# Layer 0's MLP in the one-operand form of layer 1, and two drains moved up in priority

## The chip, the cores and the metric

One core of one Trainium2 chip runs the whole program. The metric is the time of one execution in microseconds (us), the median of the runs shown. The engines are PE (TensorE matmul; its weight loads are PEld), DVE (VectorE), ACT (ScalarE), POOL (GpSimd) and SP (SyncE, which here only issues DMAs). Each engine takes its instructions in the order in which the program was built.

## The reference, cut to what matters

Two layers over 256 tokens of width 2048. The change touches the second half of layer 0:

```python
h = rmsnorm(x, norm_mlp_w[layer]) * (1.0 + sc_m) + sh_m
x = x + g_m * (jnp.square(jax.nn.relu(h @ w_ff1[layer])) @ w_ff2[layer])
```

with `w_ff1` 2048 x 8192 and `w_ff2` 8192 x 2048. The modulation vectors (`sh_m`, `sc_m`, `g_m` and their three partners of the mixer) come from `mod = silu(c) @ ada_w[layer] + ada_b[layer]`, with `ada_w` 2048 x 12288 per layer.

## The kernel before

**Precision.** A float32 product is made of three products of rounded parts: each operand is split into a high part (rounded to fp32r) and a low part (the rest), and high x low, low x high and high x high are added up. Activations are kept transposed (features on partitions, 256 tokens along the free axis), so a weight block of 128 x 128 is the stationary operand.

**Two forms of the same sum.** `mm_b` (L278 to L280) runs three matmuls of 256 columns for a block: weight high on activation low, weight low on activation high, weight high on activation high, all into one sum of 256 columns. `mm_w` (L260, L262) keeps the high and the low part of the activation side by side as one operand of 512 columns: one matmul of 512 columns with the high weights, one of 256 columns with the low weights. Its result stands as two half sums in PSUM, which whoever reads it must add. Both stream 768 columns for a block. Layer 1's MLP uses `mm_w` (`wide=True`), layer 0's uses `mm_b`.

**Weights.** They arrive in chunks of 512 KB (8 blocks, tile `raw`, 6 buffers; DMA issued on SP). ACT rounds a chunk to its high part (`wh`, L222, 3 buffers), then DVE or POOL subtracts to get the low part (`wl`, L228, 3 buffers). In layer 0 `pool_ff1` and `pool_ff` give POOL 70 to 80% of these subtractions; in the last step of FF2 and in layer 1 DVE does all.

**Modulation beside it.** `ada_w` is multiplied on DVE: each 512 KB tile `ada` (4 buffers) takes one scalar_tensor_tensor with the conditioning vector, which stands in PSUM (L309). Where its DMA stands among the weights' DMAs, and where the product stands in DVE's row, was settled when the program was scheduled. 100 of the 192 `ada` pairs are planned into layer 0's MLP.

**The MLP stage.** FF1 and FF2 are interleaved in 8 steps: step s makes 1024 hidden features (two blocks of 512), and FF2 adds the 1024 features of step s-1 to the residual `X`. In layer 0 the first 6 FF1 blocks run in two passes over 8 of the 16 contraction tiles each, so that PE can start on the first half of the normalised activations `h` (L557, L566) before the rest is made. Even before that a "lead" block (L514 to L516) runs on activations without the norm's factor, while the norm's sum is finished. The last step of FF2 is followed by the lead of layer 1, whose operands `u` are made by `lead_u` (L473, L474, L478) from `X`, and by the sum of squares `ss` (L406, L407).

**PSUM.** Results use pool `pj`, two tiles of 1024 columns, taken in turn. A tile is free for PE again when all its readers are done. With `mm_b` a tile holds 512 output features, in FF2 the sum of 32 blocks; with `mm_w` it holds 256 features, in FF2 16 blocks. FF2's readers are residual updates (scalar_tensor_tensor of 256 columns, L862 or L1124); FF1's are ACT copies or DVE adds.

**Order.** The program is written with a tile scheduler that places instructions on each engine by priority and its own estimate of when they are ready. `high_priority(offset=URGENT)` moves a piece of code ahead; it is used for the norm chains, the lead's operands and its output.

Of the kernel before, what the change touches and what calls it, by code (L numbers as in the profile page):

```python
# [12 lines left out]
ALU = mybir.AluOpType  # L13
# [6 lines left out]
KT = 16  # L20
# [24 lines left out]

CFG = [dict(wide=False, gap=1, win=[2, 2, 2, 4, 6], late=2, lead_win=False, ada_win=[4, 4, 8, 12, 14], ada_late=4, ada_out=19,
            ff1=[8, 8], ff1_blocks=6, early_ff1=[[0, 1]], stat_ff1=(0, 1), ada_ff1=[16, 16], ada_ff=68,
# [8 lines left out]
URGENT = 400  # L56
# [7 lines left out]
class Trunk:  # L64
# [840 lines left out]
    def layer(self, l):  # L905
# [6 lines left out]
        for g, kts in enumerate(G):  # L912
# [10 lines left out]
            last = kts[-1] == KT - 1  # L923
# [55 lines left out]
        nb = cfg["ff1_blocks"]  # L979
        acc = {}  # L980
        for g, kts in enumerate(G):
# [7 lines left out]
            if led:  # L989
                acc[0] = self.slot()  # L990
                if cfg["wide"]:
                    self.lead_out(ps, acc[0])
                    acc[0] = self.square_wide(acc[0])
                elif kts[-1] == KT - 1:
                    self.lead_out(ps, acc[0], AF.Relu)
                    acc[0] = self.square(acc[0])
                else:
                    self.lead_out(ps, acc[0])
# [74 lines left out]
    def ff1_wide(self, l, b, kts, acc=None):  # L1073
# [4 lines left out]
        for h in range(2):  # L1078
# [7 lines left out]
            p0, p1 = self.sums(ps)  # L1086
            if fresh:
                nc.scalar.copy(d, p1)
            else:
                nc.vector.tensor_tensor(d, p1, d, ALU.add)  # L1090
            nc.vector.tensor_tensor(d, p0, d, ALU.add)
        return self.square_wide(t) if done else t
# [13 lines left out]
    def ff2_wide(self, l, s, hid, last):  # L1106
        V = self.nc.vector
        if last:
            self.stat_begin()
            self.per = 0.0  # L1110
        tail = last and l == DEPTH - 1
        for nb in range(6 if tail else 8):
            ps = self.pair()
            for c in range(2):
# [4 lines left out]
            for n in range(2):  # L1119
                k = 2 * nb + n  # L1120
                g = self.mod[l][:, 5 * KT + k:5 * KT + k + 1]
                with self.tc.high_priority(offset=URGENT * last):
                    for c in range(n * 512, n * 512 + 512, T):
                        V.scalar_tensor_tensor(self.X(k), ps[:, c:c + T], g, self.X(k), ALU.mult, ALU.add)  # L1124
            if last and nb % 2 == 1:
                self.stat_piece(nb // 2)
            if tail:
                for n in range(2):
                    self.final_scale(2 * nb + n)
# [154 lines left out]
```

## Time and profile before

| what | value |
|---|---|
| median of 3 runs | 2505.57 us (2504.9 to 2508.94) |
| the profiled execution's own time | 2509.01 us |
| its span, first to last instruction | 2506.9 us |
| mean granted PE clock | 0.984 |
| PE / DVE / ACT / POOL busy share | 97% / 65% / 47% / 33% |
| layer 0's MLP weights issued | 504.6 to 1257.8 us |
| layer 1's MLP weights issued | from 1737.7 us to the end |

Busy shares are of the whole span. PE's matmuls overlap in the pipeline, so a busy PE is not yet PE at its full rate: its rate is read from the starts of its matmuls. In a page's row the idle time of an engine is put down to what ended it.

### The profile page before, as it was taken

What the parts mean: (1) busy time and instruction counts of PE and PEld (TensorE: products, weight loads), DVE (VectorE), ACT (ScalarE), POOL (GpSimd) and SP (SyncE); (2) the same over time, 40 slices, a digit from 0 to 9 for tenths busy, and PEclk for the clock granted to TensorE, in tenths of its full rate; (3) what the DMA queues carried; (4) which work ended last, traced back from release to release, by engine and by line L of the source; (5) the groups of instructions that cost most, each with busy time, mean ns of one, the idle gap of its engine ahead of it and who ended that gap; (6) DMA issues with size and microseconds to landing.
All of it is one profiled execution on the core that took longest, in us unless ns stands there. A gap on an engine that the chain in (4) does not pass through costs nothing.

```text
span 2506.9 us, 42898 instructions
## 1 busy us (share of the span) xinstructions
PE 2422.3 (97%) x17064; PEld 2267.9 (90%) x17064; DVE 1634.7 (65%) x2568; ACT 1178.9 (47%) x1469; POOL 822.5 (33%) x360
## 2 busy tenths in 40 slices
PE   7999999989999999999989999999999999999997
PEld 6999888989999999999989899799888888888886
DVE  5767768696655544544488777556766766676675
ACT  4444565344634444444455466454644444344443
POOL 7887665445666666676400000000000000000000
PEclk8999999989999999999999999999999999999998
DMA  9999767889999988888667777455566666666662
GB/s 347 354 331 331 274 229 272 300 319 342 323 332 339 335 295 300 300 306 302 203 237 266 264 252 268 135 177 183 170 186 187 192 186 190 188 187 189 188 192 85
DMA packets 177233, 630.22 MB, mean 251 GB/s; under 512 B 19588, under 2 KB 24326, under 8 KB 177032
## 3 DMA queue, kind: packets, MB, share of 16 engines
q1 hardware_dynamic: 176312, 626.95, 73.2%
q8 instruction: 134, 2.20, 0.4%
q10 hardware_dynamic: 720, 0.53, 0.1%
q14 instruction: 67, 0.55, 0.1%
HBM read 625.30 MB, written 2.10 MB: 250 GB/s over the span
## 4 chain that ended last, share of the span: by engine, by line
PE 72%; DVE 5%; DMA 3%; issue 1%; ACT 0%; SPq 0%; DVEq 0%; ACTq 0%
PE pj L260 18%; PE pj L279 12%; PE pj L278 12%; PE pj L280 12%; PE pj L262 9%; DMA ada<-ada_w 2%; DVE wl L228 2%; PE pj L290 1%; PE pj L289 1%; PE pj L291 1%; DVE ada L309 1%; PE mx L686 0%; DVE blk L478 0%; PE mx L515 0%; DVE h L566 0%
## 5 line engine op out<-in xcount | busy, mean ns | idle before, releaser
L222 ACT CAST wh<-raw 128x1024 fp32r<-128x1024 f32 x804 | 840.7, 1048 | 1117.0 <-PE pj L280 522.0
L228 POOL TENSOR_TENSOR wl<-raw,wh 128x1024 fp32r<-128x1024 f32 (+1 forms) x326 | 798.2, 2453 | 396.7 <-ACT wh L222 385.6
L228 DVE TENSOR_TENSOR wl<-raw,wh 128x1024 fp32r<-128x1024 f32 x478 | 587.3, 1230 | 387.7 <-ACT wh L222 386.7
L309 DVE SCALAR_TENSOR_TENSOR ada<-ada,cond 128x1024 f32<-128x1024 f32 x380 | 455.5, 1214 | 190.4 <-DMA ada<-ada_w 188.8
L279 PE MATMUL pj<-h,wl 128*128 128x256 f32 x1952 | 559.0, 287 | 7.5 <-DVE wl L228 4.2
L278 PE MATMUL pj<-h,wh 128*128 128x256 f32 x1952 | 557.5, 286 | 7.8 <-DVE h L566 6.9
L280 PE MATMUL pj<-h,wh 128*128 128x256 f32 x1952 | 555.7, 285 | 0.0
L279 PE MATMUL pj<-blk,wl 128*128 128x256 f32 x1536 | 435.5, 284 | 5.0 <-DVE wl L228 3.0
L278 PE MATMUL pj<-blk,wh 128*128 128x256 f32 x1536 | 434.8, 283 | 2.9 <-ACT blk L604 1.5
L280 PE MATMUL pj<-blk,wh 128*128 128x256 f32 x1536 | 433.9, 283 | 0.0
L1179 POOL TENSOR_TENSOR blk<-blk,R 128x1024 f32<-128x1024 f32 x1 | 2.4, 2351 | 1267.5 <-ACT R L445 1267.5
L279 PEld LDWEIGHTS pj<-h,wl 128*128 128x128 f32 x1952 | 376.9, 193 | 10.4 <-DVE wl L228 5.5
L278 PEld LDWEIGHTS pj<-h,wh 128*128 128x128 f32 x1952 | 376.2, 193 | 8.7 <-DVE h L566 7.1
L280 PEld LDWEIGHTS pj<-h,wh 128*128 128x128 f32 x1952 | 376.7, 193 | 0.2
L260 PE MATMUL pj<-blk,wh 128*128 128x512 f32 x992 | 347.4, 394 | 0.0
L260 PE MATMUL pj<-h,wh 128*128 128x512 f32 x960 | 336.7, 395 | 3.1 <-DVE h L566 3.0
L279 PEld LDWEIGHTS pj<-blk,wl 128*128 128x128 f32 x1536 | 292.5, 190 | 5.9 <-DVE wl L228 3.6
L278 PEld LDWEIGHTS pj<-blk,wh 128*128 128x128 f32 x1536 | 292.8, 191 | 3.7 <-ACT blk L604 1.7
L280 PEld LDWEIGHTS pj<-blk,wh 128*128 128x128 f32 x1536 | 292.6, 191 | 0.0
L262 PE MATMUL pj<-blk,wl 128*128 128x256 f32 x992 | 278.4, 281 | 0.0
L262 PE MATMUL pj<-h,wl 128*128 128x256 f32 x960 | 268.9, 280 | 0.0
L260 PEld LDWEIGHTS pj<-blk,wh 128*128 128x128 f32 x992 | 186.2, 188 | 43.2
(248 smaller groups left out, 2941.0 us busy)
## 6 DMA issues: line engine op xcount, KB each, us to landing
raw<-w_ff SPq DMA_DIRECT2D x508, 512.0 KB, 4.4
ada<-ada_w SPq DMA_DIRECT2D x380, 512.0 KB, 6.6
raw<-w_in SPq DMA_DIRECT2D x224, 512.0 KB, 5.3
raw<-w_out SPq DMA_DIRECT2D x64, 512.0 KB, 4.4
X<-x SPq DMA_DIRECT2D x4, 512.0 KB, 6.7
raw<-ada_w SPq DMA_DIRECT2D x4, 512.0 KB, 9.3
raw<-w_ff SPq DMA_DIRECT2D x8, 256.0 KB, 3.4
out<-blk SPq DMA_DIRECT2D x4, 512.0 KB, 2.8
```

The costliest lines, as they stand in the source:

```text
L222: nc.scalar.copy(hi, raw)
L228: eng.tensor_tensor(lo, raw, hi.bitcast(F32), ALU.subtract)
L260: nc.tensor.matmul(o.rearrange("p (a b) -> p a b", b=T), lhsT=wh[:, s], rhs=act, start=first, stop=False, skip_group_check=True)
L262: nc.tensor.matmul(o[:, :T], lhsT=wl[:, s], rhs=act[:, 0, :], start=False, stop=last, skip_group_check=True)
L278: nc.tensor.matmul(o, lhsT=wh[:, s], rhs=al, start=st, stop=False, skip_group_check=True)
L279: nc.tensor.matmul(o, lhsT=wl[:, s], rhs=ah, start=False, stop=False, skip_group_check=True)
L280: nc.tensor.matmul(o, lhsT=wh[:, s], rhs=ah, start=False, stop=last, skip_group_check=True)
L289: nc.tensor.matmul(o, lhsT=al[:, s], rhs=wh, start=first, stop=False)
L290: nc.tensor.matmul(o, lhsT=ah[:, s], rhs=wl, start=False, stop=False)
L291: nc.tensor.matmul(o, lhsT=ah[:, s], rhs=wh, start=False, stop=last)
L309: nc.vector.scalar_tensor_tensor(raw, raw, 1.0, self.cond, ALU.mult, ALU.mult, accum_out=self.part[l][:, i, h:h + 1])
L1179: nc.gpsimd.tensor_tensor(o, o, self.R[:, None, :].to_broadcast((P, 4, T)), ALU.mult)
```

## The change

`CFG[0]["wide"]` becomes true: layer 0's MLP goes through `ff1_wide`, `ff2_wide` and `lead_w2`, and its weights are laid out in chunks of 4 contraction tiles x 256 columns (the host's layout follows the flag). Bytes, chunks, the split into high and low parts and the share of POOL stay. The lead's block is no longer squared when only half of its contraction is there, POOL's share falls to 0 in FF2's last step as it did in `ff2`, and the calls of `early` that `ff2` had are put into `ff2_wide`. Besides, residual updates of every step, and FF1's half sums, are put under `high_priority` in both layers.

```diff
-CFG = [dict(wide=False, gap=1, win=[2, 2, 2, 4, 6], late=2, lead_win=False, ada_win=[4, 4, 8, 12, 14], ada_late=4, ada_out=19,
+CFG = [dict(wide=True, gap=1, win=[2, 2, 2, 4, 6], late=2, lead_win=False, ada_win=[4, 4, 8, 12, 14], ada_late=4, ada_out=19,
...
                     self.lead_out(ps, acc[0])
-                    acc[0] = self.square_wide(acc[0])
+                    if kts[-1] == KT - 1:
+                        acc[0] = self.square_wide(acc[0])
...
             p0, p1 = self.sums(ps)
-            if fresh:
-                nc.scalar.copy(d, p1)
-            else:
-                nc.vector.tensor_tensor(d, p1, d, ALU.add)
-            nc.vector.tensor_tensor(d, p0, d, ALU.add)
+            with self.tc.high_priority(offset=URGENT):
+                if fresh:
+                    nc.scalar.copy(d, p1)
+                else:
+                    nc.vector.tensor_tensor(d, p1, d, ALU.add)
+                nc.vector.tensor_tensor(d, p0, d, ALU.add)
...
         if last:
             self.stat_begin()
+            self.pool_share = 0.0
             self.per = 0.0
...
+            if last and nb >= 6:
+                self.early(CFG[l + 1]["early_win"], nb - 6, l + 1, 0, 1)
...
-                with self.tc.high_priority(offset=URGENT * last):
+                with self.tc.high_priority(offset=URGENT):
...
                 self.stat_piece(nb // 2)
+                if nb == 7:
+                    self.early(CFG[l + 1]["early_win"], 2, l + 1, 0, 1)
```

What the engines' rows look like at three places. `pj_` and a number is one PSUM tile, `ada_` one modulation tile, `wh_`/`wl_` the parts of one weight chunk, `X_91` to `X_94` the four quarters of the residual; line numbers after the change are 2 to 5 higher from L990 on.

PE in FF1, two blocks of 128 x 128 with `mm_b` before:

```order
L278 MATMUL pj_5673<-h,wh_5682 128x256
L279 MATMUL pj_5673<-h,wl_5683 128x256
L280 MATMUL pj_5673<-h,wh_5682 128x256
L278 MATMUL pj_5673<-h,wh_5682 128x256
L279 MATMUL pj_5673<-h,wl_5683 128x256
L280 MATMUL pj_5673<-h,wh_5682 128x256
```

and three blocks with `mm_w` now, so that a block takes two weight loads and not three:

```order
L260 MATMUL pj_5850<-h,wh_5881 128x512
L262 MATMUL pj_5850<-h,wl_5882 128x256
L260 MATMUL pj_5850<-h,wh_5881 128x512
L262 MATMUL pj_5850<-h,wl_5882 128x256
L260 MATMUL pj_5850<-h,wh_5881 128x512
L262 MATMUL pj_5850<-h,wl_5882 128x256
```

DVE in FF1's first pass, up to the subtraction for the twelfth weight chunk of the MLP, before:

```order
L566 TENSOR_TENSOR h<-ht_6404,h 128x2x256
L566 TENSOR_TENSOR h<-ht_6410,h 128x2x256
L557 TENSOR_TENSOR ht_6416<-X_94,R 128x512
L309 SCALAR_TENSOR_TENSOR ada_6318,part_123<-ada_6318,cond 128x1024
L557 TENSOR_TENSOR ht_6422<-X_94,R 128x512
L228 TENSOR_TENSOR wl_5890<-raw_5887,wh_5889 128x1024
```

and the same place now (L1093 is the add of a half sum, the reader of a `pj` tile):

```order
L557 TENSOR_TENSOR ht_6276<-X_94,R 128x512
L1093 TENSOR_TENSOR blk_5673<-pj_5674,blk_5673 128x512
L557 TENSOR_TENSOR ht_6282<-X_94,R 128x512
L1093 TENSOR_TENSOR blk_5673<-pj_5727,blk_5673 128x512
L309 SCALAR_TENSOR_TENSOR ada_6169,part_123<-ada_6169,cond 128x1024
L309 SCALAR_TENSOR_TENSOR ada_6172,part_123<-ada_6172,cond 128x1024
L566 TENSOR_TENSOR h<-ht_6276,h 128x2x256
L566 TENSOR_TENSOR h<-ht_6282,h 128x2x256
L309 SCALAR_TENSOR_TENSOR ada_6197,part_123<-ada_6197,cond 128x1024
L228 TENSOR_TENSOR wl_5882<-raw_5879,wh_5881 128x1024
```

Counted from the start of the norm's chain to this subtraction, DVE's row holds 14 products of `ada` and not 12, 8 of L566 and not 6, and two adds of half sums that it did not hold at all.

DVE near the end of FF2's last step, before; `pj_13922` is the last tile but one, and its four updates are one row:

```order
L309 SCALAR_TENSOR_TENSOR ada_14679,part_124<-ada_14679,cond 128x1024
L309 SCALAR_TENSOR_TENSOR ada_14682,part_124<-ada_14682,cond 128x1024
L228 TENSOR_TENSOR wl_14103<-raw_14100,wh_14102 128x1024
L862 SCALAR_TENSOR_TENSOR X_93<-pj_13922,mod_125,X_93 128x256 x4
L228 TENSOR_TENSOR wl_14157<-raw_14154,wh_14156 128x1024
L309 SCALAR_TENSOR_TENSOR ada_14685,part_124<-ada_14685,cond 128x1024
```

and now; of the last four tiles `pj_12230` is the first and `pj_12279` the second, L1129 is the residual update:

```order
L1129 SCALAR_TENSOR_TENSOR X_93<-pj_12230,mod_125,X_93 128x256
L228 TENSOR_TENSOR wl_12378<-raw_12375,wh_12377 128x1024
L407 TENSOR_TENSOR ss<-ss,blk_12226 128x512
L309 SCALAR_TENSOR_TENSOR ada_12933,part_124<-ada_12933,cond 128x1024
L309 SCALAR_TENSOR_TENSOR ada_12936,part_124<-ada_12936,cond 128x1024
L1129 SCALAR_TENSOR_TENSOR X_93<-pj_12230,mod_125,X_93 128x256 x2
L228 TENSOR_TENSOR wl_12400<-raw_12397,wh_12399 128x1024
L1129 SCALAR_TENSOR_TENSOR X_93<-pj_12279,mod_125,X_93 128x256
L228 TENSOR_TENSOR wl_12427<-raw_12424,wh_12426 128x1024
L309 SCALAR_TENSOR_TENSOR ada_12939,part_124<-ada_12939,cond 128x1024
L1129 SCALAR_TENSOR_TENSOR X_93<-pj_12230,mod_125,X_93 128x256
L309 SCALAR_TENSOR_TENSOR ada_12942,part_124<-ada_12942,cond 128x1024
```

The four updates of `pj_12230` are spread over the row, the fourth behind three subtractions and three products. The tile after next on PE, `pj_12374`, takes over the place of `pj_12230` in PSUM.

## Rows read from the trace of the kernel before

**Rows 1.** The page's first part: busy us (share of the span) xinstructions.

```profile
PE 2422.3 (97%) x17064; PEld 2267.9 (90%) x17064; DVE 1634.7 (65%) x2568; ACT 1178.9 (47%) x1469; POOL 822.5 (33%) x360
```

**Rows 2.** Stretches of the span: busy us and instructions of each engine, clock, DMA.

```profile
505.00:600.00 95.00, 82.56 (x632) 80.79 (x631) 86.68 (x136) 48.00 (x72) 47.17 (x19) 0.93 0.89 322
600.00:1240.00 640.00, 640.00 (x5373) 640.00 (x5372) 322.15 (x487) 282.00 (x276) 431.90 (x176) 1.00 0.88 308
1240.00:1320.00 80.00, 72.68 (x575) 72.06 (x574) 65.12 (x124) 42.19 (x65) 0.00 (x0) 0.93 0.66 225
1740.00:2450.00 710.00, 706.34 (x4145) 621.80 (x4144) 480.65 (x623) 317.85 (x362) 0.00 (x0) 1.00 0.61 187
```

**Rows 3.** PE in order of time: the first matmuls of four steps; start us, us.

```profile
914.62 0.28 PE L278 MATMUL pj<-blk,wh 128*128 128x256 f32 x1
...
1006.11 0.28 PE L278 MATMUL pj<-blk,wh 128*128 128x256 f32 x1
...
1899.84 0.39 PE L260 MATMUL pj<-h,wh 128*128 128x512 f32 x1
...
2078.65 0.39 PE L260 MATMUL pj<-h,wh 128*128 128x512 f32 x1
```

**Rows 4.** Groups by line and shape, 690 to 1232 us: busy us, mean ns | idle before.

```profile
L309 DVE SCALAR_TENSOR_TENSOR ada<-ada,cond 128x1024 f32<-128x1024 f32 x127 | 152.3, 1218 | 129.0 <-DMA ada<-ada_w 128.1
...
L862 DVE SCALAR_TENSOR_TENSOR X<-pj,mod,X 128x256 f32<-128x256 f32 x108 | 44.8, 477 | 59.1 <-PE pj L280 58.9
L1048 DVE TENSOR_TENSOR blk<-blk,blk 128x1024 fp32r<-128x1024 f32 x11 | 24.7, 2247 | 19.1 <-ACT blk L1047 19.1
...
L228 POOL TENSOR_TENSOR wl<-raw,wh 128x1024 fp32r<-128x1024 f32 x152 | 372.8, 2457 | 169.4 <-ACT wh L222 168.5 <-ACT mod L322 0.7
```

**Rows 5.** Groups by line and shape on DVE in layer 1's MLP, 1800 to 2440 us.

```profile
L1124 DVE SCALAR_TENSOR_TENSOR X<-pj,mod,X 128x256 f32<-128x256 f32 x224 | 102.9, 480 | 31.5 <-PE pj L262 29.7
L1091 DVE TENSOR_TENSOR blk<-pj,blk 128x512 f32<-128x512 f32 x30 | 20.5, 684 | 0.0
L1102 DVE TENSOR_TENSOR blk<-blk,blk 128x512 fp32r<-128x512 f32 x30 | 19.9, 684 | 0.0
L1097 DVE SCALAR_TENSOR_TENSOR blk<-blk 128x1024 f32<-128x1024 f32 x15 | 18.4, 1225 | 0.5
```

**Rows 6.** DVE in order of time in FF1's first pass of layer 0.

```profile
559.37 3.50 DVE L557 TENSOR_TENSOR ht<-X,R 128x512 f32<-128x512 f32 x2
...
566.29 2.37 DVE L566 TENSOR_TENSOR h<-ht,h 128x512 fp32r<-128x512 f32 x2
...
572.54 0.68 DVE L557 TENSOR_TENSOR ht<-X,R 128x512 f32<-128x512 f32 x1
573.14 1.21 DVE L228 TENSOR_TENSOR wl<-raw,wh 128x1024 fp32r<-128x1024 f32 x1
...
582.71 3.32 DVE L228 TENSOR_TENSOR wl<-raw,wh 128x1024 fp32r<-128x1024 f32 x1
```

**Rows 7.** PE's waits there and at the end of FF2 [idle before <-releaser].

```profile
578.34 0.39 PE L279 MATMUL pj<-h,wl 128*128 128x256 f32 x1 [0.79 <-POOL wl L228]
586.09 0.38 PE L279 MATMUL pj<-h,wl 128*128 128x256 f32 x1 [1.73 <-DVE wl L228]
...
1286.10 0.58 PE L515 MATMUL mx<-blk,wl 128*128 128x258 f32 x1 [4.77 <-DVE wl L228]
```

**Rows 8.** DVE in order of time before that last wait.

```profile
1264.93 1.22 DVE L309 SCALAR_TENSOR_TENSOR ada<-ada,cond 128x1024 f32<-128x1024 f32 x1 [1.23 <-DMA ada<-ada_w]
...
1282.84 2.06 DVE L478 SCALAR_TENSOR_TENSOR blk<-X,mod,blk 128x256 fp32r<-128x256 f32 x5
1284.82 1.22 DVE L228 TENSOR_TENSOR wl<-raw,wh 128x1024 fp32r<-128x1024 f32 x1
```

**Rows 9.** Stretch right behind that wait: PE busy, clock, DMA share, GB/s.

```profile
1285.20:1291.80 6.60, 5.70 (x26) 0.50 0.50 151
```

**Rows 10.** Waits of DVE, 690 to 1281 us: us in total, times, longest.

```profile
DVE ada L309 <- DMA ada<-ada_w: 129.4, 40, 8.8
```

## The prediction

> **What bounds the kernel now.** I read the page's first part, then the stretches, then PE by its starts, then DVE where PE waits. PE is busy for 97% of the span [rows 1], and in the middle of layer 0's MLP for all of it, at the full granted clock, while DVE works half the time and POOL two thirds [rows 2]. So this stretch goes at PE's rate, and time is to be won there by a shorter time for a block. At both ends of the stage it is another matter: from 505 to 600 us DVE is busy for 87 of 95 us and PE for 82.6, from 1240 to 1320 us for 65 of 80 and PE for 72.7 [rows 2]. PE waits there for low parts of weights that DVE or POOL subtract late [rows 7]. So a gain has to come from PE in the middle, and a loss from DVE at the ends. DMA engines are busy for 88% of the middle [rows 2]; a stage that is a few per cent shorter still fits.
>
> **A block on PE.** From 914.62 to 1006.11 us layer 0 runs one step of FF2 and one of FF1, 256 blocks in 91.49 us, or 357.4 ns each. From 1899.84 to 2078.65 us layer 1 runs two of both, 512 blocks in 178.81 us, or 349.2 ns [rows 3]. Both forms stream 768 columns, so the difference of 8.1 ns is that of three matmuls and weight loads against two. FF1 has 1024 blocks less the 32 that the lead takes, FF2 has 1024: 2016 x 8.1 ns = 16.4 us less. I bound this at 14 and 18: a quarter of a microsecond either way on the 91.49 us is 1 ns a block.
>
> The Trainium skill ("TensorE: Matmul & The Clock Gate", section "Wait — 56ns, not 53.3ns?") puts the fixed cost of a matmul at the full clock at about 2.5 ns whatever its length. By that, one matmul less per block would give 2016 x 2.5 ns = 5 us and no more, and the whole sum below would come out 11 us later. The rows say 8.1 ns for the pair of a matmul and its weight load, in this kernel's own operands, so the measurement decides.
>
> **What DVE takes on.** Three things, priced by layer 1's rows [rows 5] and layer 0's own [rows 4].
> - FF2's residual: a PSUM tile holds half as many features, but each has two halves, so a tile still takes four updates of 477 to 480 ns, and there are 64 tiles and not 32: 128 more updates, 0.46 us each by the group's busy time, 59 us.
> - FF1's half sums: two adds of 684 ns for a tile (one and an ACT copy in the first pass).
> - FF1's squares: L1097 and two of L1102 for a block, 1225 + 2 x 684 ns, in place of one L1048 of 2247 ns.
>
> In the middle DVE was busy for 322 of 640 us [rows 2]; with some 90 us more it is at 65%, and PE does not wait for it on average. The priorities change nothing else: in layer 1's MLP DVE's row stands in the same order as before, so I cost that part at nothing.
>
> **The middle's price.** A `pj` tile must be read before PE comes back to it. That time was some 11.4 us (32 blocks) and is now 16 x 349 ns = 5.6 us, of which the four updates take 1.9. So 3.7 us are left. DVE waits in its row for late modulation tiles: 40 times, 129.4 us in all, 3.2 us on average, 8.8 at the longest [rows 10]. Updates stand behind such products now twice as often, and sometimes between them. A mean wait just fits; a long one costs PE up to 5 us, but only if it stands ahead of a tile's readers and begins when PE has finished. I take 2 us in all, with 0 and 8 as bounds (nothing, if every wait falls between two tiles; two long ones at the upper end).
>
> **The first pass of FF1.** Here DVE is full. Its two-SBUF-input operations are slow while POOL works: two of L557 took 3.50 us at 559.37 and one 0.68 at 572.54, a subtraction 1.21 at 573.14 and 3.32 at 582.71 [rows 6]. PE waited 0.79 and 1.73 us for weights [rows 7]. After the change DVE's row holds, from the norm's chain to the subtraction that PE waited for at 586.09, two products of `ada` more (1.2 us each, [rows 4]) and three half sums (0.68): 4.4 us later, in a stretch without idle time on DVE. Those half sums are moreover what frees PSUM for PE, where an ACT copy did it before. PE therefore comes 4.4 us later out of this stretch. A PE wait of 4.77 us elsewhere was followed by 6.6 us at a granted clock of 0.50 [rows 9], which is 1.2 and not 2.4 GHz, or 3.3 us lost; the waits here (4.4 with 1.73) are about as long, so I add half of it: **6 us**. Bounds: 0, if the half sums find DVE idle; 12, if the first tile's adds wait behind all of the slow L557 and L566.
>
> **The end of FF2.** PE's last wait before layer 1 is 4.77 us [rows 7], for a subtraction that started at 1284.82 behind a train of lead operands, in a stretch that is without idle time from the modulation product at 1264.93 [rows 8]. PE went over to the lead 16 us after that product (1286.10 less the wait). The new row shows more than a longer train. The third-last tile needs the place of `pj_12230`, whose fourth update stands behind five `ada` products, three subtractions, four other updates and two adds for `ss`. From the first of the products: 5 x 1.2 + 3 x 1.2 + 5 x 0.46 + 2 x 0.6 = 13.1 us. PE wants that place 4 chunks before its old end of FF2, or 16.1 - 4 x 2.86 = 4.7 us after the product. So PE waits 8.4 us there. After that, the last chunk's subtraction stands behind a product, three updates, a dozen tiny casts (1 us together), two adds, twelve lead operands (0.41 each by the five at 1282.84, [rows 8]) and three updates: about 12 us, against two tiles' 8.4 us up to the last chunk: 3 us more. Together 11.4 in place of 4.77: **6.5 us** later. Half clock follows a wait in both cases. Bounds: 0, if the products come early enough to be done before; 10, if a second stretch at half clock follows.
>
> **Sum.** 2505.6 - 16.4 + 2 + 6 + 6.5 = 2503.7, or **2504 us** on the median. The profiled execution itself took 2509.0, 3.4 over the median, so in its own terms 2507.3. I call a change of less than 0.2% (5 us) no change, since this kernel's own runs differ by about that.
>
> **The rivals.**
> - *The ends hide it (0.34).* The half sums and updates slip into DVE's waits for `ada` tiles, of which the middle has plenty [rows 10], and the third-last tile is drained in time because the products are early. Then the 16.4 us stay but for 0 to 4: 2489 to 2494. For it: PE is at 100% over 640 us [rows 2]. Against it: the end of FF2 is full on DVE already.
> - *DVE becomes the bound in FF1's second pass (0.20), slower.* There the two tiles of a block bring four adds of half sums, one L1097 and two L1102, beside some three `ada` products and nearly one subtraction: 4 x 0.68 + 1.2 + 2 x 0.68 + 3 x 1.2 + 1 = 9.9 us of the block's 11.2. It decides from 1.4 us more per block on: 6 blocks then lose 1 to 2 us each, 6 to 12 in all, beside the ends' full price: 2511 to 2518. For it: L1048, with two SBUF inputs, took 2247 ns under POOL for what two L1102 do in 1368 without it [rows 4, 5]. The Trainium skill ("SBUF — State Buffer", section "Who interferes with whom") says that a VectorE operation with two SBUF inputs and a GpSimd operation that reads SBUF block each other for whole instructions; by that, the 48 new ones would each cost up to a POOL subtraction of 2.4 us more, and this rival would be the rule. The trace agrees on single rows, while the subtraction at 573.14 ran undisturbed [rows 6]. Against it: in the middle DVE was idle half the time [rows 2], and only 6 blocks run so.
> - *The form does not pay in layer 0 (0.06).* If chunks came at the rate of POOL's subtractions (2.46 us each [rows 4], for seven or eight chunks of ten) and not of PE, nothing would be gained in the middle, and the ends would cost: 2506 to 2518. Against it: a chunk is 2.8 us of PE, and PE does not wait in the middle [rows 2].
>
> My forecast, that both ends eat most of the gain, has 0.40, and by itself 2499 to 2510.
>
> **Chances.** Faster by over 0.2% (below 2500.6): the first rival's 0.34 and the lower edge of the forecast, 0.37. Within it: 0.39. Slower (over 2510.6): 0.24, from the second rival, part of the third and the upper edge. The range of 2490 to 2516 leaves out the best tenth and the worst tenth of these cases.
>
> **What would show it.** Starts of PE in the middle at 349 ns a block, FF2 and FF1 of a step in 89.4 us; else the first term is wrong. A PE wait of 5 us or more before or at the third chunk pair of FF1's first pass, ended by a half sum (L1093) or by a DVE subtraction. A PE wait of about 8 us at the third-last tile of FF2, ended by a residual update, and another of some 3 us before the lead. In the middle, PE waits ended by L1129 of a few microseconds in all; if they come to 10, the forecast is too fast. Layer 1's MLP from its first FF1 to the end must take what it took, or the priority is not as free as I say.

## The result: 0.8% slower

| | median us (runs) | profiled execution: own time, span, PE clock |
|---|---|---|
| before | 2506.07 (4: 2504.9 to 2508.94) | 2509.01, 2506.9, 0.984 |
| after | 2529.61 (4: 2528.14 to 2535.42) | 2535.42, 2533.6, 0.978 |

The ratio is 1.0078, with an interval from 1.0059 to 1.0097. I had forecast 2504 us, next to no change, in a range of 2490 to 2516; the kernel is slower by more than its noise and outside that range, so the prediction was wrong. The profiled execution after is the slowest of its four; its trace is 26 us behind that of before, the medians 23.5.

The first part of the page after, to be held against [rows 1]:

```profile
PE 2421.5 (96%) x15048; PEld 2173.3 (86%) x15048; DVE 1770.7 (70%) x2776; ACT 1159.3 (46%) x1478; POOL 820.4 (32%) x360
```

PE has 2016 fewer matmuls and is as busy as before: what was to be won is now waiting. DVE is busy for 136 us more (124 of them in the second row below, where I had counted some 90). The stretches after, as [rows 2], in the same order:

```profile
505.00:600.00 95.00, 75.01 (x469) 69.03 (x468) 85.17 (x138) 45.81 (x73) 38.96 (x16) 0.87 0.85 298
600.00:1240.00 640.00, 628.37 (x3553) 546.98 (x3552) 446.08 (x663) 260.44 (x281) 431.86 (x176) 0.99 0.85 307
1240.00:1320.00 80.00, 68.36 (x404) 60.60 (x402) 62.08 (x118) 35.24 (x44) 6.28 (x3) 0.96 0.61 214
1765.00:2475.00 710.00, 706.27 (x4139) 622.20 (x4138) 479.89 (x622) 317.50 (x361) 0.00 (x0) 1.00 0.57 186
```

PE is no longer busy throughout the middle, and it does less at both ends of the stage. Layer 1's MLP (last row, 25 us later) is what it was.

**Where the time went.** I read the start of the same matmul in each trace: A is the first of FF1's first pass, B the first of FF2, C the first of FF2's seventh step, D the last of layer 1's lead (L514), Z the last of the program. Before, they are at 551.20, 684.63, 1189.79, 1312.38 and 2497.30. After, they are later by:

| A | B | C | D | Z |
|---|---|---|---|---|
| +7.25 | +16.80 | +16.34 | +26.02 | +26.29 |

So 7.3 us are lost before the MLP's first pass, 9.6 in FF1's passes, 9.7 at the end of FF2, and the middle gains 0.5 where some 10 were to come. PE's longer waits at these places that the kernel before does not have, in order of time:

```profile
525.09 0.58 PE L279 MATMUL pj<-blk,wl 128*128 128x256 f32 x1 [6.83 <-DVE wl L228]
...
577.07 0.80 PE L260 MATMUL pj<-h,wh 128*128 128x512 f32 x1 [4.44 <-DVE blk L1093]
...
647.95 0.47 PE L260 MATMUL pj<-h,wh 128*128 128x512 f32 x1 [1.62 <-DVE blk L1093]
...
666.19 0.47 PE L260 MATMUL pj<-h,wh 128*128 128x512 f32 x1 [1.06 <-DVE blk L1093]
674.79 0.61 PE L319 MATMUL mx<-part,fold 128*128 128x16 f32 x2 [2.33 <-DVE ada L309]
...
850.92 0.47 PE L260 MATMUL pj<-blk,wh 128*128 128x512 f32 x1 [1.89 <-DVE X L1129]
...
1034.87 0.47 PE L260 MATMUL pj<-blk,wh 128*128 128x512 f32 x1 [1.48 <-DVE X L1129]
...
1291.83 0.77 PE L260 MATMUL pj<-blk,wh 128*128 128x512 f32 x1 [6.47 <-DVE X L1129]
...
1319.47 0.83 PE L415 MATMUL pj<-ones,ss 128*128 128x1 f32 x4 [4.19 <-DVE ss L407]
```

All are ended by DVE. Behind the wait of 4.44 us the granted clock is 0.55 from 577 to 583 us, so mostly 1.2 and not 2.4 GHz, and the first matmul of 512 columns takes 0.80 us and not 0.39; behind that of 6.47 us it takes 0.77, at a granted clock of 0.68 from 1291.8 to 1298 us. After the waits of 1 to 2 us it takes 0.47. The last wait has another origin than the rest: in front of the add for `ss` DVE itself had waited for a tile of `ada`:

```profile
1314.81 1.22 DVE L309 SCALAR_TENSOR_TENSOR ada<-ada,cond 128x1024 f32<-128x1024 f32 x1 [5.20 <-DMA ada<-ada_w]
```

**Held operations.** The first wait stands before any code that the diff touches. In DVE's row there, one product of ada stands ahead of the lead's operands (507.65) and not behind them. DVE after:

```profile
507.65 1.22 DVE L309 SCALAR_TENSOR_TENSOR ada<-ada,cond 128x1024 f32<-128x1024 f32 x1
...
509.98 4.74 DVE L474 TENSOR_TENSOR blk<-mod,blk 128x4 fp32r<-128x4 f32 x4
...
516.57 2.88 DVE L407 TENSOR_TENSOR ss<-ss,blk 128x512 f32<-128x512 f32 x1
519.37 3.39 DVE L478 SCALAR_TENSOR_TENSOR blk<-X,mod,blk 128x256 fp32r<-128x256 f32 x3
...
523.82 1.22 DVE L228 TENSOR_TENSOR wl<-raw,wh 128x1024 fp32r<-128x1024 f32 x1
```

and POOL, at the same time:

```profile
509.88 4.74 POOL L228 TENSOR_TENSOR wl<-raw,wh 128x1024 fp32r<-128x1024 f32 x2 [8.52 <-ACT wh L222]
516.52 2.38 POOL L228 TENSOR_TENSOR wl<-raw,wh 128x1024 fp32r<-128x1024 f32 x1 [1.90 <-ACT wh L222]
519.35 2.34 POOL L228 TENSOR_TENSOR wl<-raw,wh 128x1024 fp32r<-128x1024 f32 x1 [0.45 <-ACT wh L222]
```

Four operations of four columns took 4.74 us, just as long as two subtractions of POOL: two of them 2.32 and 2.35 us, the others 0.15. L407 and the first of the three L478 end 0.3 to 0.6 us behind POOL's next two. The weight's subtraction that PE needs comes behind all of it. The kernel before pays at this place too, but less: its four L474 were over before POOL began.

```profile
507.72 0.38 DVE L474 TENSOR_TENSOR blk<-mod,blk 128x4 fp32r<-128x4 f32 x4
...
511.32 2.85 DVE L407 TENSOR_TENSOR ss<-ss,blk 128x512 f32<-128x512 f32 x1
```

```profile
508.76 4.87 POOL L228 TENSOR_TENSOR wl<-raw,wh 128x1024 fp32r<-128x1024 f32 x2 [9.31 <-ACT wh L222]
```

The same in FF1's second pass of the changed kernel, DVE and then POOL:

```profile
657.85 5.73 DVE L1104 TENSOR_TENSOR blk<-blk,blk 128x512 fp32r<-128x512 f32 x2
...
666.08 1.22 DVE L1099 SCALAR_TENSOR_TENSOR blk<-blk 128x1024 f32<-128x1024 f32 x1
...
669.50 3.50 DVE L1104 TENSOR_TENSOR blk<-blk,blk 128x512 fp32r<-128x512 f32 x2
```

```profile
654.92 5.30 POOL L228 TENSOR_TENSOR wl<-raw,wh 128x1024 fp32r<-128x1024 f32 x2 [0.42 <-ACT wh L222]
660.58 2.46 POOL L228 TENSOR_TENSOR wl<-raw,wh 128x1024 fp32r<-128x1024 f32 x1 [0.36 <-ACT wh L222]
669.51 8.03 POOL L228 TENSOR_TENSOR wl<-raw,wh 128x1024 fp32r<-128x1024 f32 x3 [6.48 <-ACT wh L222]
```

Two L1104 take 5.7 us beside POOL (1.37 in [rows 5]), and L1099 takes its 1.22 where POOL is idle. Groups of DVE from 600 to 1240 us, after:

```profile
L1129 DVE SCALAR_TENSOR_TENSOR X<-pj,mod,X 128x256 f32<-128x256 f32 x212 | 97.4, 480 | 42.7 <-PE pj L262 40.0
...
L1104 DVE TENSOR_TENSOR blk<-blk,blk 128x512 fp32r<-128x512 f32 x32 | 49.1, 1562 | 5.3 <-ACT blk L1103 5.3
L1099 DVE SCALAR_TENSOR_TENSOR blk<-blk 128x1024 f32<-128x1024 f32 x16 | 33.8, 2113 | 0.5
L1093 DVE TENSOR_TENSOR blk<-pj,blk 128x512 f32<-128x512 f32 x37 | 25.4, 687 | 27.7 <-ACT blk L1090 27.5
```

What reads PSUM and SBUF (L1129, L1093) takes what it takes in layer 1, where POOL is idle. What reads SBUF twice takes 1562 for 684 and 2113 for 1225 ns.

### The profile page after: what moved, and what is told of

It is laid out like the page before. It is cut to its first block, busy times and chain, and to the rows that moved or that the text cites. A ratio compares the mean times of both kernels' runs of the same rounds, so it can differ in the third digit from the quotient of the medians.

```text
span 2533.6 us, 39042 instructions
## 1 busy us (share of the span) xinstructions
PE 2421.5 (96%) x15048; PEld 2173.3 (86%) x15048; DVE 1770.7 (70%) x2776; ACT 1159.3 (46%) x1478; POOL 820.4 (32%) x360
## 4 chain that ended last, share of the span: by engine, by line
PE 67%; DVE 9%; DMA 3%; issue 2%; ACT 1%; POOL 0%; SPq 0%; DVEq 0%; POOLq 0%; ACTq 0%
PE pj L260 33%; PE pj L262 17%; PE pj L279 3%; PE pj L278 3%; PE pj L280 3%; DMA ada<-ada_w 3%; DVE ada L309 2%; DVE wl L228 2%; PE pj L290 1%; PE pj L289 1%; PE pj L291 1%; DVE blk L1104 1%; DVE blk L478 0%; DVE X L1129 0%; DVE blk L1099 0%
## 5 line engine op out<-in xcount | busy, mean ns | idle before, releaser
L260 PE MATMUL pj<-blk,wh 128*128 128x512 f32 x2016 | 711.7, 396 | 11.1 <-DVE X L1129 10.6
L260 PE MATMUL pj<-h,wh 128*128 128x512 f32 x1952 | 690.9, 398 | 10.6 <-DVE blk L1093 7.1
L260 PEld LDWEIGHTS pj<-blk,wh 128*128 128x128 f32 x2016 | 380.3, 189 | 101.6 <-issue 9.9
L260 PEld LDWEIGHTS pj<-h,wh 128*128 128x128 f32 x1952 | 369.5, 189 | 97.8 <-DVE blk L1093 4.9
L262 PEld LDWEIGHTS pj<-blk,wl 128*128 128x128 f32 x2016 | 382.0, 189 | 3.4 <-DVE wl L228 2.7
L262 PEld LDWEIGHTS pj<-h,wl 128*128 128x128 f32 x1952 | 372.5, 191 | 1.4 <-POOL wl L228 0.8
L1129 DVE SCALAR_TENSOR_TENSOR X<-pj,mod,X 128x256 f32<-128x256 f32 x504 | 231.6, 480 | 86.9 <-PE pj L262 81.9
L278 PE MATMUL pj<-h,wh 128*128 128x256 f32 x960 | 277.1, 289 | 7.9 <-DVE h L566 5.8
L280 PE MATMUL pj<-h,wh 128*128 128x256 f32 x960 | 274.9, 286 | 0.0
L278 PEld LDWEIGHTS pj<-h,wh 128*128 128x128 f32 x960 | 186.1, 194 | 9.2 <-DVE h L566 5.9
L279 PEld LDWEIGHTS pj<-h,wl 128*128 128x128 f32 x960 | 186.4, 194 | 8.1 <-DVE wl L228 4.6
L280 PEld LDWEIGHTS pj<-h,wh 128*128 128x128 f32 x960 | 186.1, 194 | 0.2
L290 PE MATMUL pj<-wl,h 128*128 128x512 f32 x384 | 153.8, 401 | 4.3 <-DVE wl L228 4.3
```

Source lines behind the costliest of these rows:

```text
L260: nc.tensor.matmul(o.rearrange("p (a b) -> p a b", b=T), lhsT=wh[:, s], rhs=act, start=first, stop=False, skip_group_check=True)
L262: nc.tensor.matmul(o[:, :T], lhsT=wl[:, s], rhs=act[:, 0, :], start=False, stop=last, skip_group_check=True)
L278: nc.tensor.matmul(o, lhsT=wh[:, s], rhs=al, start=st, stop=False, skip_group_check=True)
L279: nc.tensor.matmul(o, lhsT=wl[:, s], rhs=ah, start=False, stop=False, skip_group_check=True)
L280: nc.tensor.matmul(o, lhsT=wh[:, s], rhs=ah, start=False, stop=last, skip_group_check=True)
L290: nc.tensor.matmul(o, lhsT=ah[:, s], rhs=wl, start=False, stop=False)
```

## The experiments

Three theories. **A**: DVE has too much to do ahead of PSUM's readers and of low parts. **B**: DVE's row stands at products whose ada tile is late. **C**: operations of DVE with two SBUF operands are held by POOL's subtractions. Kernels of one submission share a chip and the runs of the kernel before, whose median there was 2511 to 2513 us, so ratios are what compares. Delays are those of the marks against the first trace of before, in us. Each row is one execution, and those of the kernel before spread over 11 to 16 us on one chip, so a difference of 2 or 3 us between two marks is no finding by itself.

| kernel | us | ratio to before (interval) | A | B | C | D | Z |
|---|---|---|---|---|---|---|---|
| short_new | 2505.53 | 0.9965 (0.9952 to 0.9978) | -7.63 | -9.70 | -17.21 | -6.86 | -7.67 |
| short_old | 2500.13 | 0.9942 (0.9926 to 0.9958) | -5.70 | -7.86 | -7.86 | -8.23 | -9.18 |
| pool_zero | 2489.80 | 0.9900 (0.9884 to 0.9916) | -14.89 | -17.20 | -27.06 | -17.95 | -18.34 |
| pool_zero_old | 2492.36 | 0.9924 (0.9911 to 0.9938) | -14.06 | -17.27 | -17.27 | -17.70 | -20.47 |
| no_pool_early | 2543.90 | 1.0132 (1.0116 to 1.0147) | +13.71 | +25.68 | +27.36 | +32.81 | +34.03 |
| pass_mmb | 2522.88 | 1.0033 (1.0022 to 1.0044) | +6.04 | +6.58 | +5.63 | +11.43 | +15.43 |
| end_late | 2518.62 | 1.0023 (1.0011 to 1.0036) | +2.85 | +11.74 | +12.79 | +7.62 | +6.46 |
| pass_end_out | 2516.73 | 1.0019 (1.0005 to 1.0034) | -3.84 | -4.22* | +7.97 | +4.96 | +5.46 |
| square_psum | 2516.45 | 1.0016 (1.0005 to 1.0027) | +7.93 | +7.53 | -1.29 | +3.78 | +8.47 |
| c1_all | 2497.26 | 0.9935 (0.9922 to 0.9948) | -1.44 | -1.81* | -8.23 | -13.76 | -14.45 |
| c2_wide | 2497.72 | 0.9940 (0.9926 to 0.9953) | -2.79 | -6.26 | -3.84 | -8.33 | -8.81 |
| c3_pool | 2495.10 | 0.9924 (0.9906 to 0.9943) | -4.01 | -4.39* | -9.08 | -13.71 | -10.57 |
| old_fixed | 2504.57 | 0.9972 (0.9956 to 0.9988) | -2.20 | -8.07* | -0.66 | -6.13 | -6.89 |

\* Here 23 matmuls of the passes (2.7 us) stand behind B in PE's row and not ahead of it, so 2.7 us of the step from B to C belong to the passes.

The priorities needed no run: every engine's row is the same with and without them, in the kernel before as in the changed one. That half of the change does nothing, so all of the 0.8% comes with the form and with the rows that the scheduler makes for it.

### Work, or late tiles, or POOL: rows kept, one duration changed

Here the program is scheduled as it is, and then instructions are exchanged in place, so that every row keeps its order and its waits.

```diff
+    for b in nc.main_func.blocks:
+        new = []
+        for i in b.instructions:
+            if i.name in names:
...
+            new.append(i)
+        b.instructions = new
```

**short_new** (products cut to 128 columns, the rest of each left out). 

> The changed kernel, each engine's row in the same order, but each ada product issued from w_out's stage of layer 0 to the end of its MLP multiplies 128 columns of its tile and not 1024 (7/8 of these products left out; their DMAs and waits stay). A product then takes some 0.2 us and not 1.2. Theory A (DVE's work stands ahead of what frees PSUM or of low parts, so that PE waits at the ends): PE's waits before the MLP, in both passes of FF1 and at the end of FF2 all but vanish, the whole MLP gains its 16 us, and the time is 2490 to 2503. Theory B (late modulation tiles: DVE waits for their DMA while tiles of PSUM stand full): the waits of DVE for ada stay, the PE waits of FF2's end and of the middle with them, and the time is 2515 to 2527. Theory C (DVE operations with two SBUF inputs are slowed by POOL): the passes still lose 10 us or more; 2510 to 2520.

**short_old** (the same cut in the kernel before). 

> The kernel before with the same cut: products of 128 columns from w_out's stage to the end of layer 0's MLP, rows in the same order. Theory A: only the waits that are there (4.77 us at the end of FF2, 1.73 and 0.79 in the first pass, and the half clock behind them) can go, so 2495 to 2503; the difference to the changed kernel with the same cut is then the form's own gain, some 12 to 16 us. Theory B: 2503 to 2508, since the waits for late tiles stay. Theory C: 2500 to 2506.

short_new is 1.1% faster than the changed kernel, inside theory A's range by its ratio and far from theory B's, though DVE's waits for `ada` tiles grew (103.9 us from 690 to 1270 us, 74.7 in the change). So theory B falls for the loss as a whole; what stays of it is the late tile at the end of FF2, 4.38 us here with a PE wait of 3.37 behind it. From mark B to C it gains 7.5 us. But from C to D it loses 10 as the change does, and so it ends behind short_old and not 12 to 16 us ahead of it: the products that stand there are not of layer 0's MLP and were not cut, they are layer 1's. Theory C isn't told from theory A here, since a shorter product also makes room for a held operation.

**pool_zero** (POOL fills zeros, those low parts left out). 

> The changed kernel, rows in the same order, but POOL's subtractions from w_out's stage of layer 0 to the end of its MLP are replaced by POOL filling the low part with zeros (the low parts of these chunks are left out of the product). POOL then reads nothing from SBUF beside DVE. Theory C (POOL's reads slow DVE's two-input operations): L557, L566, L474, L407 fall from 1.2 to 1.8 us towards 0.7, PE's waits before the MLP and in the passes go, and the time falls by 12 to 20 us, to 2510 to 2517. Theory A (the amount of DVE's work): they fall by part only, and the time by 3 to 8 us. Theory B (late tiles): within 3 us of 2530.

**pool_zero_old** (the same in the kernel before). 

> The kernel before, rows in the same order, with POOL's subtractions from w_out's stage to the end of layer 0's MLP replaced by POOL filling zeros (those low parts are left out), as pool_zero does with the changed kernel, which took 2489.8. Theory C (the change loses up to the end of FF1's passes because its DVE order meets POOL's subtractions worse): without POOL's reads the form keeps its gain up to FF2's last step, so this kernel stays 8 to 12 us behind pool_zero there, loses 9 us less at the end of FF2, and ends within 4 us of it: 2486 to 2494. Theory A (the change loses to its own amount of DVE work): both kernels gain the same 40 us and this one ends at 2466 to 2474.

Groups of pool_zero, 600 to 1200 us. Its added lines shift the numbers: L1134 is the update, L1098 the half sum, L1109 the low part, L1104 the square.

```profile
L1134 DVE SCALAR_TENSOR_TENSOR X<-pj,mod,X 128x256 f32<-128x256 f32 x216 | 99.4, 481 | 63.7 <-PE pj L265 61.2
...
L1098 DVE TENSOR_TENSOR blk<-pj,blk 128x512 f32<-128x512 f32 x33 | 22.7, 689 | 42.1 <-ACT blk L1095 41.9
L1109 DVE TENSOR_TENSOR blk<-blk,blk 128x512 fp32r<-128x512 f32 x32 | 21.1, 687 | 5.2 <-ACT blk L1108 5.2
L1104 DVE SCALAR_TENSOR_TENSOR blk<-blk 128x1024 f32<-128x1024 f32 x16 | 19.6, 1224 | 0.5
...
L229 POOL MEMSET wl<- 128x1024 f32 x171 | 163.3, 955 | 436.4 <-ACT wh L223 434.3 <-ACT mod L325 2.0
```

With the same rows, the low part falls from 1562 to 687 ns and the square from 2113 to 1224. POOL's fill is also shorter than its subtraction, so that low parts come sooner; the durations of DVE's operations don't depend on that, the times of the marks may. The pair tells more than either: without POOL's subtractions both kernels are at B at the same time (-17.20 and -17.27), so of the 16.80 us that the change lost up to there none is left (one wait of 2.1 us in the first pass stays, about what the form saves in the passes). From B to C the form gains 9.9 us, nearly its full rate, and from C to D it gives back 9.5 of them, with POOL idle at the wait there (7.4 us for an update). That agrees with theory C up to mark C, and something else is behind it. pool_zero's gain over the change, 40 to 45 us, is more than twice what I had expected, and the kernel before gains some 17 us up to B by the same exchange: it pays to POOL's subtractions as well.

**no_pool_early**, `pool_out` and `pool_ff1` at 0 and nothing left out. 

> The changed kernel with no subtraction on POOL in w_out's stage and in FF1's passes of layer 0 (DVE does them all, nothing left out). Theory C (what costs is that DVE and POOL hold each other up): L474 takes 0.1 us each and L407 0.7, and the start of FF2 comes 5 to 15 us earlier than in the changed kernel though DVE has some 25 subtractions of 1.2 us more: 2515 to 2525. Theory A (the amount of DVE's work): 30 us more work on an engine that is busy for 85 to 90% there makes it later by 10 to 20 us: 2540 to 2550.

Its four L474 took 0.38 us and L407 0.69, as theory C says of durations, and yet it is slower, at the lower edge of theory A's range: from 600 to 710 us DVE is busy for 106.8 of 110 us. So POOL can't be spared here; the two have to be kept apart by what they read.

### The two ends

**pass_mmb**: the passes of the six early blocks on `mm_b`. 

> The changed kernel with the two passes of FF1's first six blocks on mm_b again (three matmuls of 256 columns, a whole tile of 512 features drained by one ACT copy or one DVE add), everything else of layer 0's MLP on mm_w. Theory A with its loss in the passes: the 5 us of the first pass and the 10 us of the second go, the 352 blocks give up 3 us of gain, so 2515 to 2519; the losses of the middle and of FF2's end stay. Rival (the half sums are not what makes the passes late, the order of the rows is): 2526 to 2533.

```diff
-                acc[b] = ff1(l, b, kts, acc.get(b))
+                acc[b] = (self.ff1_pass if len(G) > 1 else ff1)(l, b, kts, acc.get(b))
```

(`ff1_pass`, not shown, is FF1's pass with `mm_b`.) From A to B it loses 0.5 us and not 9.6. The middle gains 1 us, as little as in the change, and FF2's end still loses (5.8). The loss of the passes is bound to `mm_w` there.

**end_late**: layer 1's first products later. 

> The changed kernel, with the first eight pairs of ada products of layer 1's mixer stage issued some three blocks later, so that none of them stands in DVE's row among the last residual updates of layer 0's FF2. Theory A (what stands ahead of the fourth update of a tile at FF2's end is products of layer 1's stage, placed there by the scheduler): the PE wait of 6.75 us and the 9 us lost between the last FF1 block and layer 1 go down to 0 to 2 us, 2521 to 2524 beside 2530. Rival (the end is bound by the two halves' updates and the lead's operands themselves): less than 3 us come back, 2527 to 2533.

```diff
             self.pump_until(l, 0, kts[-1])
+            if l > 0:
+                self.credit = -8.0
```

In the change, DVE's row at FF2's end holds these products between a tile's updates; PE's wait of 6.47 us ended with the update at 1291.20:

```profile
1279.32 1.22 DVE L309 SCALAR_TENSOR_TENSOR ada<-ada,cond 128x1024 f32<-128x1024 f32 x1
...
1284.34 1.22 DVE L309 SCALAR_TENSOR_TENSOR ada<-ada,cond 128x1024 f32<-128x1024 f32 x1
...
1285.47 1.22 DVE L309 SCALAR_TENSOR_TENSOR ada<-ada,cond 128x1024 f32<-128x1024 f32 x1
...
1290.06 1.22 DVE L309 SCALAR_TENSOR_TENSOR ada<-ada,cond 128x1024 f32<-128x1024 f32 x1
...
1291.20 0.48 DVE L1129 SCALAR_TENSOR_TENSOR X<-pj,mod,X 128x256 f32<-128x256 f32 x1
```

In end_late from C to D 5.2 us are gained where the change lost 9.7, no wait of PE for an update is left there but one of 1.5 us, and the wait for `ss` is 0.4 us. That layer 1's products in this place cost the end is shown, and more came back than expected. Two effects go together: products between updates (theory A) and the late tile (theory B); the run doesn't tell their shares apart.

The run gave something unasked. Up to FF2's last tiles its rows are those of the changed kernel, and yet mark A stands at +2.85 and not +7.25. DVE, and then POOL, of end_late at the place of the first wait:

```profile
510.06 4.71 DVE L474 TENSOR_TENSOR blk<-mod,blk 128x4 fp32r<-128x4 f32 x4
...
516.63 0.68 DVE L407 TENSOR_TENSOR ss<-ss,blk 128x512 f32<-128x512 f32 x1
517.24 1.26 DVE L478 SCALAR_TENSOR_TENSOR blk<-X,mod,blk 128x256 fp32r<-128x256 f32 x3
```

```profile
509.96 4.72 POOL L228 TENSOR_TENSOR wl<-raw,wh 128x1024 fp32r<-128x1024 f32 x2 [8.30 <-ACT wh L222]
518.12 2.62 POOL L228 TENSOR_TENSOR wl<-raw,wh 128x1024 fp32r<-128x1024 f32 x1 [3.44 <-ACT wh L222]
```

L407 began in a gap of POOL and took 0.68 us, not 2.88; the three L478 took 1.26, not 3.39. The same instructions in the same order cost 4.3 us more or less by whether they meet POOL.

**pass_end_out**: both, and `ada_out` at 14. 

> Three repairs in one kernel, read apart by their places: the passes of FF1 on mm_b (as pass_mmb), layer 1's first products later (as end_late), and 14 ada pairs in w_out's stage of layer 0 and not 19, so that fewer products stand between lead operands. If the places add up: no loss before the MLP (7 us in the changed kernel), none in the passes, none at FF2's end, and 8 to 10 us of the form's gain stay: 0.3 to 0.5% faster than the kernel before on the same chip (ratio 0.995 to 0.997). If the loss before the MLP is a chance meeting of DVE with POOL, it can as well stay: ratio 0.998 to 1.001.

No loss before A and none at the end, as hoped, but the places don't add up: from B to C it loses 9.5 us (12.2 less the 2.7 of the note). PE waits five times for residual updates from 690 to 1270 us, 15.1 us in all and 5.0 at the longest, there with the update behind a square of 2.32 us and two low parts of 4.58. So in the middle too the loss looks like theory C's. Why these waits are longer than in the changed kernel, with the same squares, is open.

### What is held, read from PSUM

**square_psum**: the square goes through a PSUM tile, so that no operation of FF1's blocks reads SBUF twice. 

> The changed kernel, squares of layer 0's FF1 made another way: ACT does relu and writes the square of each half into a PSUM tile, ACT rounds it from there, and DVE subtracts the low part with one operand in PSUM; L1099 and the two L1104 with both operands in SBUF are gone. Theory C (DVE is held by POOL only in operations that read two SBUF operands): the low parts take 0.68 us each beside POOL, PE's waits at the first tiles of FF2's steps (2.16 and 1.76 us) go, the middle gains 8 to 10 us on the kernel before and not 0.5, the second pass loses 3 to 6 us and not 10; in all 8 to 15 us faster than the changed kernel, 9 to 16 slower than the kernel before. Theory A (DVE's amount of work): 11 blocks lose 1.2 us of DVE work each, and 0 to 4 us come back. Rival (ACT becomes late with high parts of weights): no faster than the changed kernel.

```diff
-        nc.vector.scalar_tensor_tensor(t, t, 0.0, t, ALU.max, ALU.mult)
+        if self.in_psum:
+            nc.scalar.activation(t, t, AF.Relu)
...
+            if self.in_psum:
+                q = self.bank((P, 2, T))
+                nc.scalar.activation(q, t[:, 2 * h:2 * h + 2, :], AF.Square)
             s = self.slot((P, 2, 2, T), F32R)
-            nc.scalar.copy(s[:, 0], t[:, 2 * h:2 * h + 2, :])
-            nc.vector.tensor_tensor(s[:, 1], t[:, 2 * h:2 * h + 2, :], s[:, 0].bitcast(F32), ALU.subtract)
+            nc.scalar.copy(s[:, 0], q)
+            nc.vector.tensor_tensor(s[:, 1], q, s[:, 0].bitcast(F32), ALU.subtract)
```

(`in_psum` is set in layer 0.) Low part and POOL's subtraction in square_psum, 600 to 1240 us, from the groups of either engine, and last POOL's in the changed kernel:

```profile
L1112 DVE TENSOR_TENSOR blk<-mx,blk 128x512 fp32r<-128x512 f32 x32 | 21.4, 686 | 16.1 <-ACT blk L1111 16.1
```

```profile
L228 POOL TENSOR_TENSOR wl<-raw,wh 128x1024 fp32r<-128x1024 f32 x179 | 432.7, 2418 | 197.9 <-ACT wh L222 193.9 <-ACT mod L322 3.1 <-DVE blk L1094 0.4
```

```profile
L228 POOL TENSOR_TENSOR wl<-raw,wh 128x1024 fp32r<-128x1024 f32 x176 | 433.3, 2465 | 208.2 <-ACT wh L222 204.5 <-DMA ada<-ada_w 3.3 <-ACT mod L322 0.4
```

POOL works as much as before, and the low part takes 686 ns. From A to B it gains 0.4 us (the change lost 9.6), from B to C 8.8 (the change 0.5). The middle is within what theory C said, the passes and the whole (0.6% faster than the change, 0.2% behind the kernel before) came out better than it said, and far outside theory A's 0 to 4 us. The first pass's wait for a half sum stays (4.35 us), so that one isn't the squares'; the second pass's waits go. The wait at FF2's end stays (6.66 us), as it must. This shows theory C, for the second pass and the middle, with nothing left out of the computation. Behind D this kernel and pass_mmb lose 4 to 5 us more, with a PE wait of 5.21 us for layer 1's normalised activations (1.52 in the kernel before); no run here looks into that.

**c1_all**: pass_end_out and square_psum together. 

> Squares in PSUM, passes on mm_b, layer 1's first products later, 14 pairs of ada in w_out's stage: pass_end_out with the squares of square_psum. Theory C: pass_end_out lost 12.7 us from the start of FF2 to its end, nearly all in five PE waits at first tiles of FF2's steps; these go and the 10 us of the form's own gain in the middle show: 14 to 20 us faster than the kernel before at FF2's end, 0.5 to 0.8% faster on the median. Theory A: 1 to 4 us better than pass_end_out, ratio 1.000 to 1.002.

**c2_wide**: the same, passes on `mm_w`. 

> As c1_all, but with FF1's passes on mm_w as in the change. If the squares were what POOL held in the second pass, the passes now lose 0 to 3 us and this is as fast as c1_all or 2 us faster; if the half sums and the norm's own two-operand operations (L557, L566) are, the passes lose 5 to 10 us and it is that much slower than c1_all.

**c3_pool**: c1_all, `pool_ff` at 0.9. 

> c1_all with POOL's share of the subtractions in the middle at 0.9 and not 0.8. DVE's subtractions (held to 3.25 us where they meet POOL's) are half as many. If POOL at 2.4 us for a subtraction keeps up with 0.9 of PE's chunks of 2.8 us: within 2 us of c1_all. If it falls behind: PE waits for low parts from POOL, 3 to 20 us slower.

**old_fixed**: the kernel before with these repairs. 

> The kernel before (mm_b throughout layer 0's MLP) with the repairs of c1_all that apply to it: squares of FF1 through PSUM, layer 1's first products later, 14 ada pairs in w_out's stage. If the form is worth its 10 us in the middle once DVE no longer waits for POOL (as pool_zero beside pool_zero_old says), the repairs alone give 2 to 8 us, ratio 0.997 to 0.999, and c1_all (0.9935) stays ahead by 8 to 12 us. If the repairs do it all: ratio 0.993 to 0.995.

The first three beat both kernels by their ratios. c1_all is 0.65% faster than the kernel before (13.8 us at D, just short of the 14 expected), and from B to C it gains 9.1 us (6.4 and the 2.7 of the note) where pass_end_out lost 9.5. c2_wide ties with it: from A to B it gains 3.5 us, where c1_all loses 2.3 by the same note, so `mm_w` costs the passes nothing any more; but a wait of 5.7 us follows at FF2's first tiles, for an update that stands in DVE's row behind a square that ACT is late with. c3_pool isn't told apart from c1_all by its interval, and its PE doesn't wait for POOL in the MLP's passes and middle. old_fixed gains 0.28%, so c1_all is ahead of it by some 0.37% (9 us, from two chips). How much of that is the form's alone is open: with these repairs `mm_b` loses 4.7 us from B to C by the same note, 3.5 of them in two waits for DVE's low parts of weights, and the repairs weren't fitted to it.

## Why the prediction was wrong

**The step that failed** is the price of what DVE takes on: I took L1097 (now L1099) and the two L1102 (now L1104) at 1225 and 684 ns from [rows 5], a stretch in which POOL stands idle, and carried them into one in which POOL is busy for two thirds of the time [rows 2]. They measured 2113 and 1562. The same hold falls on operations that I gave no price at all (L474, L407, L478 before the MLP). I had the opposite in hand: the L1048 of 2247 ns and the 3.50 us of two L557 [rows 4, 6], and the rule of the Trainium skill ("SBUF — State Buffer", section "Who interferes with whom"): a VectorE operation with two SBUF inputs and a GpSimd operation that reads SBUF exclude each other, while one that only writes doesn't, nor a VectorE operation with at most one SBUF input outside the 2-port performance modes. By that rule my second rival "would be the rule", and I gave it 0.20. The traces agree with it in the groups shown: 1562 and 687 ns for the same operation beside POOL's subtraction and beside its fill, 480 and 481 ns for the residual update, which has one operand in PSUM.

**Point by point.**
- *A block on PE*, 8.1 ns: nearly right. Starts of PE in the middle after, a step of FF2 and one of FF1 apart:

```profile
932.45 0.40 PE L260 MATMUL pj<-blk,wh 128*128 128x512 f32 x1
...
1022.02 0.39 PE L260 MATMUL pj<-blk,wh 128*128 128x512 f32 x1
```

  That is 89.57 us for 256 blocks where no wait falls, 7.5 ns a block less than before; I had said 89.4. Of the Trainium skill's 2.5 ns per matmul ("TensorE: Matmul & The Clock Gate", section "Wait — 56ns, not 53.3ns?") this pair of a matmul and its weight load is three times, as the rows of before had said.
- *The middle's price*, 2 us within 0 to 8: mis-sized, it was some 9.4 (9.9 in pool_zero's pair less 0.5). I looked for late ada tiles; it was held squares, which square_psum shows.
- *The first pass of FF1*, 6 us: its wait for a half sum came, 4.44 us at 577.07, with the half clock behind it. Ahead of that sum stand an L566 of 2.02 and an L557 of 1.69 us beside POOL (0.69 undisturbed) and two products. My count of three half sums was wrong: up to the subtraction that I named, the row shown before holds two, and two L566 that I left out. *The second pass*, priced only in the rival, is where the rest of the 9.6 us from A to B went. With the 2.6 us that the form saves on these 352 blocks both passes cost 12.2. The rival (2511 to 2518) had the place and the cause; its time was still too low, for it left the middle and the row before the MLP as they were.
- *The end of FF2*, 6.5 us within 0 to 10: it measured 9.7, and 11.6 with the 1.9 us that the form saves on the last 256 blocks, so it was outside its bounds. The first wait came as described (6.47 for the fourth update of the third-last tile, where I had 8.4; the 16.1 us in that sum are 16.4 by the rows, which makes it 8.1). Where I had 3 us more before the lead for the last chunk's subtraction, there came 4.19 inside the lead for `ss`, behind a late tile of `ada`. What I missed is that the five products are layer 1's and can be sent later, which end_late does.
- *Before the MLP*: no term at all. One product of ada (1.2 us) stands ahead of the lead's operands, and L474 falls into POOL's subtractions: 7.25 us in the profiled execution, 2.85 in end_late's with the same rows. How it falls in the executions without a profile isn't recorded, so whether it makes the difference between the trace's 26 us and the medians' 23.5 stays open.
- *The priorities*, free: right, and more than that, they move nothing.
- *Layer 1's MLP* took what it took: 706.27 us of PE in 710.

In sum: 7.25 + 9.55 - 0.46 + 9.68 + 0.27 (behind D) = 26.3 us in the trace, where I had -16.4 + 2 + 6 + 6.5 = -1.9. Of the 28 us between the two some 7 lie before the MLP, 6 in the passes, 7 to 8 in the middle, 5 at the end of FF2 and 1 in the size of the block's gain (7.5 for 8.1 ns).

## What to carry to other kernels

Take the duration of an operation from a stretch in which the same neighbours are at work; for VectorE beside GpSimd count the SBUF operands of each, and let one of them come from PSUM where both are at work. A change that halves what a PSUM tile holds leaves its readers half the time, and their waits can become PE's, so look at what stands ahead of the reader in its engine's row, work of the next stage included. And compare the rows with and without a priority before giving it a price.

## What was not expected of the hardware

An operation of four columns can cost 2.3 us: two of the four L474 took as long as the subtraction of POOL that had begun just before them (0.10 and 0.05 us), the two others 0.15. With the same rows, such meetings made 4.3 us of difference between an execution of the change and one of end_late at one place. In the other direction POOL is hardly slowed on the mean: its subtraction has a mean of 2465 ns with the held squares and 2418 without.
